# Twenty slots in place of seventeen in the shared pool, and a smaller scratch region for dynamic transfers

## The chip, the cores and the metric

The kernel runs on one core of one Trainium2 chip. The metric is the device time of one execution in microseconds (us), the median of several runs. Engines are named as the profile names them: PE (matrix products), PEld (its weight loads), DVE (vector), ACT (scalar), POOL (GpSimd) and SP (which here issues DMA transfers).

## The reference

Two layers work on 512 tokens of 1024 channels in float32. Layer 0 mixes tokens with RWKV-7, layer 1 with a spatial gating unit (SGU); a SwiGLU network (FFN, 2816 hidden channels) follows each, and every sub-layer has a norm before and after it.

```python
def step(S, inp):                                   # RWKV-7, for each of 16 heads of 64 channels
    r_t, w_t, k_t, v_t, a_t, b_t = inp
    sa = jnp.einsum('bhij,bhj->bhi', S, a_t)
    S = (S * w_t[:, :, None, :]
         + sa[..., None] * b_t[:, :, None, :]
         + v_t[..., None] * k_t[:, :, None, :])
    y = jnp.einsum('bhij,bhj->bhi', S, r_t)
    return S, y
...
for i in range(DEPTH):                              # DEPTH = 2
    h = _rmsnorm(x, norm_gains[i, 0])
    h = _rwkv7_time_mix(h, ...) if i % N_MIXERS == 0 else _sgu_mixer(h, ...)
    x = x + _rmsnorm(h, norm_gains[i, 1])
    h = _rmsnorm(x, norm_gains[i, 2])
    h = (jax.nn.silu(h @ w_gate) * (h @ w_up)) @ w_down
    x = x + _rmsnorm(h, norm_gains[i, 3])
```

## The kernel before

The four sub-layers run one after the other: RWKV from 0 to about 430 us, FFN0 to about 690, SGU to about 960, FFN1 to the end at 1313.6. Every large product is made of three matmuls (`mm3`, L206): the float32 operands are split into a high half (cast on ACT, L181, `whi`) and a low half (subtraction on DVE, L182, `wlo`).

RWKV handles the heads in four blocks of four heads (256 channels). Instead of a loop over tokens it takes chunks of 64 tokens. A string fixes in which order the steps are written down, and a scheduler of the language then sets the order on each engine from what depends on what, so that the steps overlap:

```python
PLAN = "P0 E0 P1 E1 P2 E2 P3 E3 X0 F0 B0 F1 V0 V1 V2 V3 B1 S0 F2 S1 F3 N0 B2 N1 B3 S2 N2 S3 N3".split()
```

The letters that matter here, each with the number of its block:

- X prepares the mixed input of the v-projection (`xsp`, four buffers of the shared pool), and V is that projection (`v`, PE, L206); its results go to memory (`Vd`, L868).
- F ("front") loads `MV` (L988) and `ST` (L982), multiplies them (`lm`, PE, L1004) and transposes `ST` (`bkt`, PE, L1018). ACT copies the results into `MV`, `BX` and `LA`, POOL masks them (L972).
- B ("back") inverts triangular matrices. DVE transposes `LA` to `LX` (L1035), runs 15 steps that fill `Dm` (`tm`, L1049, and `Dm`, L1051), and transposes `Dm` twice (`hn` L1054 and `Dt` L1055). Then PE and the copying engines alternate: `Qp` (PE, L1071), `Qs` (DVE, L1074), `Np` and `Tp` (PE, L1080, L1083), `Dn` (ACT, L1086), `bdT` (ACT and DVE, L1088), `Q2p` (PE, L1094), `Q` (ACT and DVE, L1097, L1098), `T2p` (PE, L1103), `bdT` (ACT and DVE, L1107). At its end PE makes `mp` (L1112) and `gh` (L1119), and DVE writes eight pairs of `MV` from them (L1121, L1122). PE also transposes `MV` in it (`mvt`, L1062).
- S scans the eight chunks: `us` and `Yp` on PE (L1148, L1161), the next state `su` on DVE and ACT (L1150, L1153), its v part loaded from `Vd` on SP (L1133).
- N finishes a block: group norm (`mu` L1177, `Y` L1179, `va` L1183, `nr` L232 to L237, `Y` L1185), the bonus (`hn`, L1195, `vt`, PE, L1198), the output gate (`g2x` L1212, `g2l` L182, `yt`, PE, L1223, `ob` on DVE, L1224 and L1228). The finished `ob` goes to memory (`od`, L1237) and comes back as `oraw` (L1281), which is split into `oT` (L181, L182) for the output projection.

Below, "block 2" means B2, the second block counted from 0 being B1; `mp(2)` is block 2's first `mp`.

Many tiles of all sub-layers share one pool of equal buffers ("slots", 4 KB in each of the 128 partitions):

```python
    def slot(self, shape, dt, name, tag="s"):
        ...
        return self.sp.tile(shape, dt, name=name, tag="s", bufs=SLOTS)
```

From this pool come four `MV` and four `BX` for each block (`BX` is free at the end of B, `MV` at the end of S), the four `xsp`, `oraw` and `oT`, the eight `hT` that each norm writes, and in an FFN its activations (`act`) and the blocks of its down projection (`ablk`, `actw`). A tile that finds no free slot is written only after the last reader of the slot's earlier tile. X0, F0 and F1 together ask for 4 + 8 + 8 = 20.

POOL issues nine transfers itself, with 512 KB each (the rows `gain` of the norms, L243, and `wsr`, L1306). For such transfers the program keeps a scratch region in every partition, 16,384 bytes by default. All other transfers are issued by SP.

Of the kernel before, what the change touches and what calls it, by code (L numbers as in the profile page):

```python
# [29 lines left out]
BANKS_F0 = dict(tr=(1, 2), gu=(3, 4, 7, 6), R=(3, 4), Q=(5, 0), Z=(7, 6), h0=(1, 2, 4, 0), h1=(3, 5, 7, 6))  # L30
BANKS_SGU = dict(tr=(1, 2), pa=(3, 5, 7, 6), h0=(1, 2, 4, 0), h1=(3, 5, 7, 6))
BANKS_F1 = dict(tr=(1, 2), gu=(4, 0, 7, 6), R=(4, 0), Q=(3, 5), Z=(7, 6), h0=(1, 2, 0, 5), h1=(4, 3, 7, 6))
SLOTS = 17
E2 = 7
PLAN = "P0 E0 P1 E1 P2 E2 P3 E3 X0 F0 B0 F1 V0 V1 V2 V3 B1 S0 F2 S1 F3 N0 B2 N1 B3 S2 N2 S3 N3".split()
XV = "xxxessss"
# [96 lines left out]
class Trunk:  # L133
# [41 lines left out]
    def slot(self, shape, dt, name, tag="s"):  # L175
        if tag == "x":
            return self.sx.tile(shape, dt, name=name, tag="x", bufs=XSLOTS)
        return self.sp.tile(shape, dt, name=name, tag="s", bufs=SLOTS)

# [1252 lines left out]
```

## Time and profile before

| what | value |
|---|---|
| median of 3 runs | 1320.23 us (1316.43 to 1321.08) |
| the profiled execution | 1315.28 us, span 1313.6 us, mean PE clock 0.984 |
| PE busy | 1257.4 us (96%) |
| DVE busy | 988.1 us (75%) |
| ACT busy | 739.4 us (56%) |
| POOL busy | 151.6 us (12%) |
| transfers issued by POOL | 1296 packets, 4.72 MB |

The times of the trace are counted from the start of the span. A row of the timeline gives start, duration, engine, line, operation, output and inputs, the number of instructions and, in brackets, how long the engine had been idle before and what ended that. A row of the windows gives for a stretch its length, the busy time of PE, PEld, DVE, ACT and POOL with the number of instructions, the clock that was granted to PE (1.00 is full), the share of the DMA engines and GB/s. In the PE rows one `lm` of the program shows as two instructions.

### The profile page before, as it was taken

To read this page: it belongs to the slowest core of one execution; us is meant where nothing else is said; L and a number is where in the kernel's file an instruction comes from. 1 tells how busy PE (TensorE), PEld (TensorE's weight loads), DVE (VectorE), ACT (ScalarE), POOL (GpSimd) and SP (SyncE) were. 2 spreads that over 40 slices of the span, in tenths; PEclk is the share of its full clock that TensorE was granted. 3 is DMA by queue.
4 is the path that set the end of the run, shared out by engine and by line. 5 is a ranking of instruction groups with operands and counts; after the bars stand their busy time and mean duration, and the time that the engine had idled before them with its cause. 6 is when DMAs were issued, how large, how long until landed. Compare 5 with 4: busy or idle time off the path is not lost.

```text
span 1313.6 us, 24404 instructions
## 1 busy us (share of the span) xinstructions
PE 1257.4 (96%) x9644; PEld 1091.1 (83%) x9644; DVE 988.1 (75%) x1613; ACT 739.4 (56%) x1303; POOL 151.6 (12%) x300
## 2 busy tenths in 40 slices
PE   5999999989899899999999999999989999999998
PEld 3667799978787698999997878878888999998876
DVE  7976766477866687868779977476679877789985
ACT  7986785686444463445546556543454454556553
POOL 0000284566000002100000000020002000000000
PEclk9999999999979999999999999999989999999999
DMA  5137594322243225244344314343430433444322
GB/s 163 34 95 175 146 224 156 88 72 65 75 127 112 75 80 160 68 126 125 92 154 136 122 49 128 94 135 94 144 97 1 129 98 105 120 125 149 113 65 81
DMA packets 219379, 144.29 MB, mean 110 GB/s; under 512 B 67920, under 2 KB 193408, under 8 KB 219264
## 3 DMA queue, kind: packets, MB, share of 16 engines
q1 hardware_dynamic: 217968, 138.01, 36.4%
q0 software_dynamic: 1296, 4.72, 1.1%
q8 instruction: 76, 1.25, 0.4%
q14 instruction: 39, 0.32, 0.1%
HBM read 128.54 MB, written 14.16 MB: 109 GB/s over the span
## 4 chain that ended last, share of the span: by engine, by line
PE 68%; DVE 7%; ACT 2%; issue 1%; DMA 1%; POOL 0%; DVEq 0%; ACTq 0%
PE acc L206 25%; PE Q L206 10%; PE gu L206 9%; PE R L206 7%; PE Z L206 7%; PE u L206 3%; DVE wlo L182 1%; PE gh L1119 1%; PE mp L1112 1%; PE Yp L1161 1%; PE lm L1004 1%; DVE wsum L405 1%; DVE x L336 1%; PE s L1366 1%; PE ptr L281 0%
## 5 line engine op out<-in xcount | busy, mean ns | idle before, releaser
L182 DVE TENSOR_TENSOR wlo<-wraw,whi 128x1024 fp32r<-128x1024 f32 x83 | 103.1, 1244 | 66.5 <-ACT whi L181 57.7
L206 PE MATMUL Q<-bc,whi 128*128 128x256 f32 x816 | 147.3, 281 | 2.2 <-ACT hn L449 2.2
L206 PE MATMUL acc<-whi,ablk 128*128 128x512 f32 x448 | 141.6, 395 | 2.7 <-DVE acc L623 2.7
L181 ACT CAST whi<-wraw 128x1024 fp32r<-128x1024 f32 x83 | 86.9, 1050 | 101.5 <-PE acc L206 29.2
L206 PEld LDWEIGHTS Q<-bc,whi 128*128 128x128 f32 x816 | 125.5, 189 | 2.8 <-ACT hn L449 2.6
L181 ACT CAST whi<-wsum 128x1024 fp32r<-128x1024 f32 x68 | 71.1, 1051 | 85.0 <-PE Q L206 24.3
L206 PE MATMUL gu<-hT,whi 128*128 128x256 f32 (+1 forms) x448 | 112.0, 342 | 3.3 <-ACT hT L62 1.7
L206 PE MATMUL Q<-bc,wlo 128*128 128x256 f32 x408 | 114.6, 281 | 0.0
L206 PEld LDWEIGHTS acc<-whi,ablk 128*128 128x128 f32 x448 | 84.2, 188 | 23.3 <-ACT hn L621 1.8
L206 PE MATMUL Z<-bc,whi 128*128 128x256 f32 x544 | 99.8, 281 | 0.0
L206 PE MATMUL R<-bc,whi 128*128 128x256 f32 x544 | 98.7, 281 | 0.0
L182 DVE TENSOR_TENSOR wlo<-wsum,whi 128x1024 fp32r<-128x1024 f32 x68 | 82.2, 1221 | 21.5 <-ACT whi L181 20.4
L181 ACT CAST whi<-wq 128x1024 fp32r<-128x1024 f32 x51 | 53.5, 1050 | 72.3 <-PE R L206 22.9
L206 PEld LDWEIGHTS gu<-hT,whi 128*128 128x128 f32 x448 | 78.8, 197 | 13.7 <-ACT hT L62 2.4
L206 PE MATMUL acc<-wlo,ablk 128*128 128x512 f32 x224 | 88.5, 395 | 1.5 <-DVE wlo L182 1.5
L182 DVE TENSOR_TENSOR wlo<-wq,whi 128x1024 fp32r<-128x1024 f32 x51 | 65.3, 1284 | 27.6 <-ACT whi L181 27.4
L206 PEld LDWEIGHTS Z<-bc,whi 128*128 128x128 f32 x544 | 84.1, 189 | 0.0
L206 PEld LDWEIGHTS R<-bc,whi 128*128 128x128 f32 x544 | 83.8, 188 | 0.2
L206 PE MATMUL proj<-xsp,whi 128*128 128x512 f32 x256 | 82.4, 401 | 1.3 <-ACT r L813 1.3
L206 PEld LDWEIGHTS Q<-bc,wlo 128*128 128x128 f32 x408 | 77.2, 189 | 0.0
L206 PE MATMUL Z<-bc,wlo 128*128 128x256 f32 x272 | 76.3, 282 | 0.9 <-DVE wlo L182 0.9
L206 PE MATMUL R<-bc,wlo 128*128 128x256 f32 x272 | 76.6, 282 | 0.0
(377 smaller groups left out, 3191.7 us busy)
## 6 DMA issues: line engine op xcount, KB each, us to landing
wc<-in_ffn_w_down_dram SPq DMA_DIRECT2D x38, 512.0 KB, 3.9
wq<-in_ffn_w_gate_dram SPq DMA_DIRECT2D x68, 256.0 KB
wq<-in_ffn_w_up_dram SPq DMA_DIRECT2D x68, 256.0 KB, 4.7
wraw<-in_rwkv_w_rkv_dram SPq DMA_DIRECT2D x24, 512.0 KB, 5.3
wraw<-in_sgu_w_in_dram SPq DMA_DIRECT2D x16, 512.0 KB, 4.3
wraw<-in_ffn_w_gate_dram SPq DMA_DIRECT2D x10, 512.0 KB
wraw<-in_ffn_w_up_dram SPq DMA_DIRECT2D x10, 512.0 KB, 3.9
x<-in_x_dram SPq DMA_DIRECT2D x8, 512.0 KB, 3.6
```

The lines of the kernel that those rows point to most:

```text
L181: self.nc.scalar.copy(hi, src)
L182: self.nc.vector.tensor_tensor(lo, src, hi.bitcast(F32), op=ALU.subtract)
L206: self.nc.tensor.matmul(out, l, r, start=start, stop=stop, skip_group_check=resumed)
L336: v.scalar_tensor_tensor(xts[tt][:, c], f, y[:, 0:1], xts[tt][:, c], op0=ALU.mult, op1=ALU.add)
L405: v.tensor_tensor(s, x, y, op=ALU.add)
L1004: mm(lm[:, cc * P:(cc + 1) * P], st[:, cc].rearrange("p n t -> p (n t)"), mv[:, cc, :, hd, :], start=True, stop=True)
L1112: mm(mp[:, cc * P:(cc + 1) * P], bdT[:, q * NC + 4 * hh + cc].rearrange("p h t -> p (h t)"), mt[:, cc, :], start=True, stop=True)
L1119: mm(gh[:, cc * P:(cc + 1) * P], mt[rows, cc, :], bx[rows, 0:2, cc, :], start=True, stop=True)
L1161: mm(yp[yr, yc], MV[hh, q][:, cc, 1, hd, :], su[:, q, hd, :], start=True, stop=True)
L1366: mm(acc[:, tt * P:(tt + 1) * P], vt[tt][:, m * P:(m + 1) * P], wsT[:, m, :], start=True, stop=True)
```

## The change

Two numbers change: the pool has 20 slots, and the scratch region has 4,096 bytes in each partition. The region gives up 12 KB of a partition, and three more slots take 12 KB.

```diff
-SLOTS = 17
+SLOTS = 20
...
-    nc = bacc.Bacc("TRN2", target_bir_lowering=False, num_devices=1)
+    nc = bacc.Bacc("TRN2", target_bir_lowering=False, num_devices=1, dynamic_dma_scratch_size=4096)
```

No operation is added or removed, but the scheduler sets another order from about 200 us on. Three places follow.

DVE behind block 0's inversion, before. `bdT<-T2p` is the end of the inversion, the `MV` pairs follow `gh`, and `LX` opens block 1.

```order
L1098 COPY Q_1947<-Q2p 32x512
L1107 COPY bdT<-T2p 32x16x32
L1121 TENSOR_TENSOR MV<-gh,BX 128x4x64
L1122 TENSOR_TENSOR MV<-gh,MV 128x4x64
L1121 TENSOR_TENSOR MV<-gh,BX 128x4x64
L1122 TENSOR_TENSOR MV<-gh,MV 128x4x64
L1121 TENSOR_TENSOR MV<-gh,BX 128x4x64
L1122 TENSOR_TENSOR MV<-gh,MV 128x4x64
L1035 STREAM_TRANSPOSE LX<-LA 128x1024
```

The same place in the changed program:

```order
L1098 COPY Q_1947<-Q2p 32x512
L1107 COPY bdT<-T2p 32x16x32
L1035 STREAM_TRANSPOSE LX<-LA 128x1024
L1049 TENSOR_TENSOR tm<-LX,Dm 128x2x15
L1051 TENSOR_TENSOR Dm<-Dm,tm 128x2x15
```

`LX` of block 1 now follows `bdT` directly, ahead of all eight `MV` pairs of block 0.

DVE at block 2, before, from the last transpose of `Dm`. The `LX` near the end is that of block 3, `ob` and `g2x` belong to N0 and N1, `su` to the scan of block 1.

```order
L1054 STREAM_TRANSPOSE hn<-Dm 128x32x32
L1055 STREAM_TRANSPOSE Dt<-Dm 128x32x32
L1228 TENSOR_TENSOR ob<-gate,ob 128x512
L1212 TENSOR_TENSOR g2x<-g2r,g2x 32x256
L1150 TENSOR_TENSOR su<-us,pc 64x2x64
L1074 TENSOR_TENSOR Qs<-Qp,id_144 128x512
L182 TENSOR_TENSOR g2l<-g_4806,g2h 128x256
L1150 TENSOR_TENSOR su<-us,pc 64x2x64 x3
L1035 STREAM_TRANSPOSE LX<-LA 128x1024
```

The same place in the changed program:

```order
L1055 STREAM_TRANSPOSE Dt<-Dm 128x32x32
L1150 TENSOR_TENSOR su<-us,pc 64x2x64
L1035 STREAM_TRANSPOSE LX<-LA 128x1024
L1228 TENSOR_TENSOR ob<-gate,ob 128x512
L1212 TENSOR_TENSOR g2x<-g2r,g2x 32x256
L1049 TENSOR_TENSOR tm<-LX,Dm 128x2x15
L1051 TENSOR_TENSOR Dm<-Dm,tm 128x2x15
L1150 TENSOR_TENSOR su<-us,pc 64x2x64
L1049 TENSOR_TENSOR tm<-LX,Dm 128x2x28
L1051 TENSOR_TENSOR Dm<-Dm,tm 128x2x14x2
L1049 TENSOR_TENSOR tm<-LX,Dm 128x2x39
L1074 TENSOR_TENSOR Qs<-Qp,id_144 128x512
```

Block 3's `LX` and its first steps now stand ahead of block 2's `Qs`.

PE at the end of block 2's inversion, before, up to its first `mp`:

```order
L1018 MATMUL bkt<-ident,ST 128x128 x4
L1094 MATMUL Q2p<-Dn_4024,LA 32x32
L1062 MATMUL mvt<-ident,MV 128x128 x4
L1094 MATMUL Q2p<-Dn_4024,LA 32x32 x18
L1062 MATMUL mvt<-ident,MV 128x128 x8
L1103 MATMUL T2p<-bdT,Q_4064 32x32 x19
L1062 MATMUL mvt<-ident,MV 128x128 x4
L1103 MATMUL T2p<-bdT,Q_4064 32x32 x13
L1198 MATMUL vt<-ident,hn 128x128 x4
L1062 MATMUL mvt<-ident,MV 128x128 x8
L1198 MATMUL vt<-ident,hn 128x128 x4
L1112 MATMUL mp<-MVt,bdT 128x128 x4
```

The same place in the changed program:

```order
L1083 MATMUL Tp<-Dt,Qs 32x32 x64
L1094 MATMUL Q2p<-Dn_4024,LA 32x32 x32
L1198 MATMUL vt<-ident,hn 128x128 x4
L1103 MATMUL T2p<-bdT,Q_4064 32x32 x32
L1198 MATMUL vt<-ident,hn 128x128 x4
L1112 MATMUL mp<-MVt,bdT 128x128 x4
```

The `mvt` and the last `bkt` have moved ahead of `Tp`; eight `vt` are what is left between its steps. From this `mp` on the rest of RWKV keeps its order on PE. In the same way the last 12 `lm` and 8 `bkt` of F1 move from behind block 0's first `mp` into the v-projection ahead of it, and on SP six loads of block 2's `MV` (L988) now stand ahead of the last two stores of `Vd`. The down projections of both FFNs keep more blocks of their input at once, and the first gate and up products of FFN1 stand in another order among the transposes (`ptr`, L281) of its norm.

## Prediction

> **What bounds the kernel now.** I read the page first, for the engine that carries the chain, then windows by stage, for the stages in which that engine is not full.
>
> ```profile
> span 1313.6 us, 24404 instructions
> PE 1257.4 (96%) x9644; PEld 1091.1 (83%) x9644; DVE 988.1 (75%) x1613; ACT 739.4 (56%) x1303; POOL 151.6 (12%) x300
> PE 68%; DVE 7%; ACT 2%; issue 1%; DMA 1%; POOL 0%; DVEq 0%; ACTq 0%
> 240.00:289.00 49.00, 44.34 (x807) 39.57 (x806) 32.12 (x73) 35.95 (x91) 31.91 (x76) 0.97 0.37 104
> 460.00:690.00 230.00, 227.51 (x1710) 217.35 (x1711) 181.03 (x238) 112.05 (x169) 15.86 (x12) 0.99 0.40 115
> 950.00:980.00 30.00, 26.39 (x170) 24.00 (x169) 25.69 (x94) 19.19 (x63) 2.36 (x4) 0.89 0.41 117
> 1190.00:1280.00 90.00, 88.68 (x400) 72.28 (x400) 85.24 (x105) 53.89 (x74) 0.00 (x0) 1.00 0.34 103
> ```
>
> PE is busy 1257.4 of 1313.6 us and no instruction is added or removed, so the change can only move the 56.2 us in which PE is idle, and the stretches in which its clock is below 1. The order changes only from about 200 us on. In the stages with a new order PE is idle 2.5 us (FFN0), 3.6 (into FFN1), 1.3 (down projection of FFN1), and 4.7 in the 49 us that hold RWKV's blocks 0 and 1. Slots are missed in one place:
>
> ```profile
> SPq L988 <- DVE MV L1121: 23.5, 5, 11.3
> ```
>
> SP's loads of `MV` wait 23.5 us, up to 11.3 at once, until DVE has written block 0's `MV` and so freed `BX`. For PE that matters where its queue runs dry or slows:
>
> ```profile
> 225.00:230.00 5.00, 3.31 (x241) 3.03 (x241) 1.37 (x2) 1.73 (x3) 0.00 (x0) 1.00 0.14 54
> 230.00:235.00 5.00, 5.00 (x56) 4.83 (x51) 0.70 (x1) 1.89 (x4) 2.00 (x5) 0.66 0.01 3
> 285.00:290.00 5.00, 4.44 (x24) 4.29 (x24) 4.55 (x9) 4.12 (x9) 3.48 (x7) 0.66 0.00 0
> ```
>
> Idle are 1.7 us at 225 to 230; the clock of 0.66 costs (1 - 0.66) x 5 = 1.7 us in each of the other two.
>
> **The scratch region: 0.** It serves only the transfers that POOL issues.
>
> ```profile
> q0 software_dynamic: 1296, 4.72, 1.1%
> L243 POOL DMA_DIRECT2D gain<-in_norm_gains_dram x4: 528/606/691, 387.5 to 1173.1; - x4
> ...
> L243 POOL DMA_DIRECT2D gain<-in_sgu_ln_b_dram x1: 528/528/528, 860.6 to 860.6; - x1
> L243 POOL DMA_DIRECT2D gain<-in_sgu_bs_dram x1: 577/577/577, 870.5 to 870.5; - x1
> ```
>
> There are nine, moving 1.1% of the engines' time, and two close ones are 870.5 - 860.6 = 9.9 us apart. If a smaller region made POOL wait before each until the last had gone, it would wait in idle time (12% busy). If it split a transfer in two, one would cost a second issue, 0.6 us, hidden there. Bounds 0 and 9 x 0.6 = 5.4 if every one were exposed; I take 0, since POOL has 88% to spare.
>
> **Blocks 0 and 1: PE gets up to 8 us ahead.** Rows of DVE and PE before:
>
> ```profile
> 236.80 0.69 DVE L1107 COPY bdT<-T2p 32x512 f32<-32x512 f32 x1 [4.99 <-ACT bdT L1107]
> 243.47 0.42 DVE L1121 TENSOR_TENSOR MV<-gh,BX 128x256 f32<-128x256 f32 x1 [5.99 <-PE gh L1119]
> 250.42 1.98 DVE L1035 STREAM_TRANSPOSE LX<-LA 128x1024 f32<-128x1024 f32 x1
> 236.07 0.66 PE L1018 MATMUL bkt<-ident,ST 128*128 128x128 f32 x4
> 281.23 2.09 PE L1004 MATMUL lm<-MV,ST 128*128 128x128 f32 x16
> 285.56 1.77 PE L1112 MATMUL mp<-MVt,bdT 128*128 128x128 f32 x8 [2.24 <-DVE bdT L1107]
> ```
>
> F1's last 12 `lm` (24 instructions at 2.09/16 = 0.13 us: 3.1) and 8 `bkt` (0.66/4 = 0.165: 1.3) move into the v-projection, 4.4 us. So block 0's `bdT` ends at 236.80 + 0.69 + 4.4 = 241.9 at the latest, and `LX` of block 1 starts right there, with `LA` already made, instead of at 250.42: 8.5 us earlier, or 10.1 if the 1.7 us gap takes part of the 4.4. `LX` leads to `mp(1)` at 285.56 in 35.1 us, and on the way PE drops 16 of F2's instructions, 2.1 us. `mp(1)` then comes at 275 to 277. PE cannot gain more than its idle 4.7 and 1.7 and the two clock losses, 2 x 1.7: 9.8. I take 8.
>
> **Block 2: most of it is given back, because DVE is full.**
>
> ```profile
> 289.00:313.10 24.10, 24.10 (x304) 20.67 (x303) 22.54 (x57) 13.94 (x36) 14.52 (x34) 0.99 0.22 54
> 288.63 1.38 DVE L1185 TENSOR_TENSOR Y<-Y,nr_y 128x1024 f32<-128x1024 f32 x1
> 290.32 1.98 DVE L1035 STREAM_TRANSPOSE LX<-LA 128x1024 f32<-128x1024 f32 x1 [0.31 <-POOL LA L972]
> 292.34 0.42 DVE L1121 TENSOR_TENSOR MV<-gh,BX 128x256 f32<-128x256 f32 x1
> 298.26 0.41 DVE L1122 TENSOR_TENSOR MV<-gh,MV 128x256 f32<-128x256 f32 x1
> 311.18 1.93 DVE L1055 STREAM_TRANSPOSE Dt<-Dm 128x1024 f32<-128x1024 f32 x1
> 312.97 0.67 DVE L1228 TENSOR_TENSOR ob<-gate,ob 128x512 f32<-128x512 f32 x1
> 313.66 0.43 DVE L1212 TENSOR_TENSOR g2x<-g2r,g2x 32x256 fp32r<-32x256 f32 x1
> 315.17 0.69 DVE L1074 TENSOR_TENSOR Qs<-Qp,id 128x512 f32<-128x512 f32 x1 [0.76 <-PE Qp L1071]
> 328.23 0.69 DVE L1088 COPY bdT<-Tp 32x512 f32<-32x512 f32 x1
> 337.38 0.69 DVE L1107 COPY bdT<-T2p 32x512 f32<-32x512 f32 x1
> 338.12 1.16 PE L1112 MATMUL mp<-MVt,bdT 128*128 128x128 f32 x8 [0.52 <-DVE bdT L1107]
> ```
>
> Four `MV` pairs of block 1 now precede `LX` of block 2 on DVE. Before, the fourth pair ended at 298.67, 13.1 us behind `mp(1)`; added to 275 to 277 that gives 288.1 to 290.1 for `LX(2)`: 1.2 us gained of 290.32 in the middle, and not 8. From `LX(2)` to the end of `Dt` took 313.11 - 290.32 = 22.8. Out go four pairs (8 x 0.37 = 3.0), in come the last steps of N0's norm (1.4 for `Y`, about 1.2 for five small ones): 22.4. `Dt` ends at 289.1 + 22.4 = 311.5, 1.6 earlier.
>
> Then `Qs` waits behind `LX` of block 3 (2.0), `ob` (0.7), `g2x` (0.4), two `su` (0.6) and five small `tm`, `Dm` (0.2, 0.2, 0.4, 0.2, 0.5): 5.2, to 316.7, where it stood at 315.17, 1.5 later. Here the price is the order itself, since `Qp` is early. From `Qs` to the second `bdT` (L1088) DVE has by the new order 24 instructions, whose durations in the trace sum to 13.4 with `Qs`, where before it took 328.92 - 315.17 = 13.75: 330.1. From there to `bdT` (L1107) stand 6.1 us, where before 338.07 - 328.92 = 9.2 went, because N1's norm now comes earlier. `bdT` ends at 336.2, 1.9 us earlier, and `mp(2)` with it. I take -2; the bounds are -8 (all that PE gained is kept) and +2 (`Qs` alone decides).
>
> **Behind `mp(2)`: 0.** The order on PE is unchanged and PE is full.
>
> ```profile
> 338.10:356.50 18.40, 17.74 (x168) 15.22 (x168) 17.70 (x45) 7.03 (x17) 0.00 (x0) 1.00 0.10 33
> 356.50:380.00 23.50, 20.16 (x541) 17.74 (x540) 9.17 (x17) 11.66 (x26) 0.41 (x2) 0.64 0.35 97
> 365.00:370.00 5.00, 4.92 (x100) 4.56 (x102) 2.44 (x5) 2.27 (x6) 0.41 (x2) 0.50 0.02 4
> ```
>
> A new hole is the price to bound: `mvt` and `bkt` no longer fill block 2's inversion, so PE stands idle there while DVE works: 24 `mvt` alone, at `bkt`'s 0.165, are 4.0 us. If the clock is 0.66 for 5 us behind it, as it was at 230, that is 1.7; if nothing, 0. The clock of these rows bears on it: 0.66 follows a short gap at 229, 0.50 stands at 365 where PE is busy 4.92 of 5.
>
> [...]
>
> **The other stages: -0.5.** In FFN0's down projection and at the start of FFN1 PE waited for what more slots might bring earlier:
>
> ```profile
> 706.65 0.50 PE L206 MATMUL acc<-wlo,ablk 128*128 128x512 f32 x1 [1.45 <-DVE wlo L182]
> 960.12 0.66 PE L281 MATMUL ptr<-ident,x 128*128 128x128 f32 x4 [2.50 <-DVE hT L64]
> ```
>
> The first waits for a weight, which no slot brings: 0, bounds -1.5 and +2 (by the 1.3 us idle in FFN1's twin, doubled for a worse order). In the second more `gu` products stand ahead of the transposes; -0.5, bounds -2.5 and +2.
>
> Sum: 0 - 2 + 0 - 0.5 = -2.5 on the profiled execution's 1315.28 us, 1312.8. The median shown is 4.95 us above that execution; on it the sum gives 1317.7, rounded 1317.5. A difference of 0.5%, 6.6 us, is about what a measurement of this kernel can tell from none.
>
> **Rivals.** (a) The lead of 8 us is kept. For it speaks that PE carries 68% of the chain and DVE waited 4.99 and 5.99 us at block 0; against it the 22.54 of 24.1 us of DVE. It needs DVE to catch up at block 2 by letting the norm's rows overlap; with the 9.8 of the bound and 0.5 it gives 1320.2 - 9 = 1311.
>
> (b) Slower: the round trip of `ob`. On ACT and DVE the two splits of block 0's `oT` now stand inside block 2's inversion, ahead of the `bdT` copy, and wait for a transfer there and back.
>
> ```profile
> 353.66 0.68 DVE L1228 TENSOR_TENSOR ob<-gate,ob 128x512 f32<-128x512 f32 x1
> 361.79 1.14 ACT L181 CAST oT<-oraw 128x512 fp32r<-128x512 f32 x2 [2.80 <-DMA oraw<-od]
> ```
>
> In block 1's trip 361.79 - 354.34 = 7.5 us passed. Block 0's second `ob` ends at about 314.6 by the steps above, so `oraw` is there at 322.1; DVE reaches `oT` 7 us behind `Qs`, at 323.7. With 1.6 us to spare it costs nothing; each us more is a us on `mp(2)`. If the load queues behind SP's loads of `su` as long as the longest wait above, 11.3, mp(2) is 9.7 later: 1320.2 - 2.5 + 9.7 = 1327.
>
> (c) Nothing comes of the slots: DVE's order costs at `Qs` what was gained, and the hole's clock takes the rest: -2 + 1.7, 1320.
>
> **Chances.** Forecast 0.42, (c) 0.20, (a) 0.25, (b) 0.13. Faster by over 0.5%: (a), and a little of the forecast's own spread, 0.28; slower: (b), 0.13; within: 0.59. The range takes in (a) with the full 9.8 and some of (b): 1308 to 1325. The likeliest case alone spans 1314 to 1321.
>
> **What would show it.** Right: `LX` of block 1 at 240 to 242, no wait of L988 for `MV`, `mp(1)` at 275 to 277, `Qs(2)` at 316 to 318, `mp(2)` at 335 to 337, PE idle ahead of it for 4 us or more. Wrong: `mp(2)` before 332 (a), ACT waiting for `oraw` before it (b), or a wait of POOL ahead of L243, for the scratch.

## The result: 0.8% slower

| | before | after |
|---|---|---|
| median | 1317.94 us (5 runs, 1314.71 to 1321.08) | 1328.10 us (5 runs, 1326.07 to 1330.81) |
| profiled execution: span, mean PE clock | 1313.6 us, 0.984 | 1324.3 us, 0.979 |
| PE idle in the span (1 minus busy) | 56.2 us | 62.9 us |

The ratio is 1.0082 with a 95% interval of 1.0064 to 1.0100: the changed kernel lies 10 us behind, outside the range of 1308 to 1325, and on the other side of the old time from the 1317.5 forecast.

The page of the changed kernel gives busy times that are almost those of before. Nothing was added; the time went into idling and into a slower clock.

```profile
span 1324.3 us, 24399 instructions
PE 1261.4 (95%) x9644; PEld 1095.7 (83%) x9644; DVE 987.7 (75%) x1613; ACT 737.9 (56%) x1303; POOL 151.7 (11%) x300
PE 76%; DVE 12%; ACT 5%; issue 3%; DMA 2%; SPq 1%; POOL 0%; DVEq 0%; ACTq 0%
```

In the chain that ended last, DVE has risen from 7% to 12%, ACT from 2% to 5% and issue from 1% to 3%. That rise is no sign of the loss: the shares before add up to 79% only, because that chain could be followed back no further than to 270 us, and the one after reaches the start. Where the time went is read from the same marks in both traces. The last mark is the start of the last product of RWKV's output projection.

| us from the start of the span | before | after | later by |
|---|---|---|---|
| `LX` of block 1 (DVE) | 250.4 | 243.4 | -7.0 |
| last `su` of block 0's scan (DVE) | 271.6 | 287.1 | 15.5 |
| first `mp` of block 1 (PE) | 285.6 | 287.1 | 1.5 |
| `LX` of block 2 (DVE) | 290.3 | 300.8 | 10.5 |
| `Qp` of block 2 (PE), first to last | 311.4 to 315.1 | 321.8 to 327.8 | 10.4 to 12.7 |
| `Qs` of block 2 (DVE) | 315.2 | 328.7 | 13.5 |
| first `mp` of block 2 (PE) | 338.1 | 346.0 | 7.9 |
| last product of RWKV's output projection | 453.9 | 463.7 | 9.8 |
| end of the span | 1313.6 | 1324.3 | 10.7 |

The lead of 7 us that the prediction expected at block 1's `LX` is there. It is gone at block 1's `mp`, has become a loss of 10 at block 2's `LX`, and all but 0.9 of the loss has arisen by the end of RWKV. How far such marks scatter is seen in the traces of the first two experiments below, in which RWKV has the order of before: `LX` of block 2 at 292.6 and 290.5, `mp` of block 2 at 341.1 and 338.5, the last product at 456.3 and 465.0. So less than 3 us at a mark of block 1 or 2 tells nothing, and at the last product one trace can be 11 us late without a new order. That the loss itself is there rests on the medians of the runs. Two places explain the rows up to block 2's `mp`.

**First place: the scan of block 0 and block 1's inversion in one queue.** `Qp` of block 1 needs `hn`. From `LX` to the end of `hn` DVE takes 18.1 us before and 18.3 after, but before, `Qp` begins 0.2 us behind that end,

```profile
266.42 2.12 DVE L1054 STREAM_TRANSPOSE hn<-Dm 128x1024 f32<-128x1024 f32 x1
268.69 1.28 PE L1071 MATMUL Qp<-hn,LA 32*32 32x32 f32 x128 [0.47 <-DVE hn L1054]
271.61 0.28 DVE L1150 TENSOR_TENSOR su<-us,pc 64x128 f32<-64x128 f32 x1 [0.56 <-ACT su L1153]
```

and after, at 266.65, 5.0 us behind it: on PE a `Yp` of block 0's scan stands ahead of `Qp` and waits for `su`, which stands on DVE behind `hn` and `Dt`, and 16 `lm` follow.

```profile
259.65 2.03 DVE L1054 STREAM_TRANSPOSE hn<-Dm 128x1024 f32<-128x1024 f32 x1
263.31 0.25 DVE L1150 TENSOR_TENSOR su<-us,pc 64x128 f32<-64x128 f32 x1
263.61 0.33 PE L1161 MATMUL Yp<-su,MV 128*64 128x64 f32 x2 [2.00 <-DVE su L1150]
263.87 2.85 PE L1004 MATMUL lm<-MV,ST 128*128 128x128 f32 x16
```

The timeline of DVE after, from block 1's `LX` on: the scan's last states and what ended DVE's wait for them, then block 1's `MV` pairs and block 2's `LX`.

```profile
243.38 2.04 DVE L1035 STREAM_TRANSPOSE LX<-LA 128x1024 f32<-128x1024 f32 x1 [1.72 <-POOL LA L972]
278.42 0.28 DVE L1150 TENSOR_TENSOR su<-us,pc 64x128 f32<-64x128 f32 x1 [2.07 <-PE us L1148]
284.23 0.28 DVE L1150 TENSOR_TENSOR su<-us,pc 64x128 f32<-64x128 f32 x1 [4.80 <-PE us L1148]
287.06 0.28 DVE L1150 TENSOR_TENSOR su<-us,pc 64x128 f32<-64x128 f32 x1 [1.84 <-PE us L1148]
291.61 0.42 DVE L1121 TENSOR_TENSOR MV<-gh,BX 128x256 f32<-128x256 f32 x1 [4.27 <-PE gh L1119]
297.77 0.42 DVE L1121 TENSOR_TENSOR MV<-gh,BX 128x256 f32<-128x256 f32 x1 [0.97 <-PE gh L1119]
298.11 0.41 DVE L1122 TENSOR_TENSOR MV<-gh,MV 128x256 f32<-128x256 f32 x1
299.57 1.28 DVE L1195 TENSOR_TENSOR hn<-hn,bn 128x512 f32<-128x512 f32 x2
300.77 1.98 DVE L1035 STREAM_TRANSPOSE LX<-LA 128x1024 f32<-128x1024 f32 x1
```

PE in the same stretch:

```profile
266.65 1.82 PE L1071 MATMUL Qp<-hn,LA 32*32 32x32 f32 x120
277.20 0.76 PE L1094 MATMUL Q2p<-Dn,LA 32*32 32x32 f32 x36 [1.91 <-issue]
277.89 0.45 PE L1148 MATMUL us<-su,MV 128*64 128x64 f32 x8
282.62 1.19 PE L1103 MATMUL T2p<-bdT,Q 32*32 32x32 f32 x62
```

DVE waits for `us`, and `us` stands on PE behind `Q2p` and `T2p` of block 1. Before, six of the scan's seven steps ran ahead of block 1's `Qp` on PE and the seventh ahead of `Np`; after, three run ahead of it and four between the steps of the inversion, which begins 7 us earlier. Each chain needs the answer of another engine after every step, and in one queue it also waits for the other's answers and for the `lm` between them. `LX` to `mp` of block 1 takes 43.7 us in place of 35.1, and the scan ends 15.5 us later.

`LX` of block 2 then begins 13.7 us behind block 1's `mp`, where it began 4.8 us behind it. Three things come ahead of it: four `MV` pairs of block 1 that now stand ahead of it on DVE, the last of them released by `gh` at 297.77; two instructions of block 0's norm (`va`, `hn`), which starts only behind its scan; and block 2's `LA`, whose last mask ended at 297.2 and not at 290.3, since F2's `lm` stand in the same queue of PE. This trace doesn't tell which of the three would do alone.

**Second place: block 2's filling work ahead of its inversion.** In the changed kernel `mvt` and the last `lm` and `bkt` stand before or between the pieces of `Qp`, which takes 6.0 us and not 3.7. Its first and last pieces before,

```profile
311.38 0.89 PE L1071 MATMUL Qp<-hn,LA 32*32 32x32 f32 x80
...
314.74 0.38 PE L1071 MATMUL Qp<-hn,LA 32*32 32x32 f32 x20
```

and after, with some of the `mvt`:

```profile
321.20 0.60 PE L1062 MATMUL mvt<-ident,MV 128*128 128x128 f32 x4
321.81 0.73 PE L1071 MATMUL Qp<-hn,LA 32*32 32x32 f32 x62
...
323.86 0.66 PE L1062 MATMUL mvt<-ident,MV 128*128 128x128 f32 x4
...
327.42 0.38 PE L1071 MATMUL Qp<-hn,LA 32*32 32x32 f32 x20
```

Behind `Qp` PE runs dry:

```profile
335.66 0.25 PE L1083 MATMUL Tp<-Dt,Qs 32*32 32x32 f32 x3 [1.96 <-issue]
340.43 1.12 PE L1198 MATMUL vt<-ident,hn 128*128 128x128 f32 x4 [3.26 <-DVE hn L1195]
345.99 2.07 PE L1112 MATMUL mp<-MVt,bdT 128*128 128x128 f32 x8 [1.28 <-DVE bdT L1107]
```

For the gap of 1.96 us the trace shows nothing that PE waited for ("issue"). Such gaps stand in runs of 32x32 products of the kernel before, too (1.53 us at 229.46, 1.47 at 364.48), so its reason stays open; at the other two PE waits for DVE.

The windows of 5 us from 335, first before, then after:

```profile
335.00:340.00 5.00, 4.20 (x26) 3.72 (x24) 4.77 (x16) 1.96 (x3) 0.00 (x0) 0.79 0.02 3
340.00:345.00 5.00, 4.64 (x39) 3.94 (x40) 4.80 (x17) 1.10 (x2) 0.00 (x0) 1.00 0.00 0
345.00:350.00 5.00, 5.00 (x47) 4.24 (x46) 4.96 (x10) 2.08 (x4) 0.00 (x0) 1.00 0.13 52
```

```profile
335.00:340.00 5.00, 1.51 (x67) 1.37 (x66) 4.94 (x10) 2.11 (x3) 0.00 (x0) 0.66 0.41 122
340.00:345.00 5.00, 4.08 (x72) 3.21 (x72) 4.87 (x17) 2.19 (x5) 0.00 (x0) 0.50 0.02 3
345.00:350.00 5.00, 4.01 (x18) 3.68 (x19) 4.77 (x10) 1.03 (x2) 0.00 (x0) 0.50 0.00 0
```

PE idles 3.5 us of the first stretch while DVE is full (4.94 of 5), and for the 10 us behind it the granted clock is half. The eight instructions of `mp` take 2.07 us, where they took 1.16 before. Idle time, and busy time multiplied by what the clock lacks to 1, come to 10.0 us between 335 and 350 (5.4 and 4.6), and in the kernel before to 2.0. That is an estimate from the mean clocks of these windows, but it is most of the 10 us. From `Qs` to `mp` the changed kernel is the faster one, 17.3 us against 23.0, since the filling work is done by then.

### The profile page after: what moved, and what is told of

The parts are those of the page before. It is cut to its first block, busy times and chain, and to the rows that moved or that the text cites. A ratio compares the mean times of both kernels' runs of the same rounds, so it can differ in the third digit from the quotient of the medians.

```text
span 1324.3 us, 24399 instructions
## 1 busy us (share of the span) xinstructions
PE 1261.4 (95%) x9644; PEld 1095.7 (83%) x9644; DVE 987.7 (75%) x1613; ACT 737.9 (56%) x1303; POOL 151.7 (11%) x300
## 4 chain that ended last, share of the span: by engine, by line
PE 76%; DVE 12%; ACT 5%; issue 3%; DMA 2%; SPq 1%; POOL 0%; DVEq 0%; ACTq 0%
PE acc L206 22%; PE Q L206 9%; PE gu L206 9%; PE R L206 7%; PE Z L206 6%; PE proj L206 5%; PE u L206 3%; PE v L206 2%; PE lm L1004 2%; DVE wlo L182 2%; PE gh L1119 2%; PE mp L1112 1%; PE Yp L1161 1%; ACT whi L181 1%; ACT xs L765 1%
## 5 line engine op out<-in xcount | busy, mean ns | idle before, releaser
L206 PEld LDWEIGHTS gu<-hT,whi 128*128 128x128 f32 x448 | 78.8, 197 | 13.5 <-DVE hT L64 2.6
```

Of the source, the lines that this page charges most:

```text
L206: self.nc.tensor.matmul(out, l, r, start=start, stop=stop, skip_group_check=resumed)
```

## The experiments

The kernels of one group ran on one chip, with runs of the kernel before among them; ratios are to those. In the diffs `issue_after(x)` places what it wraps behind `x` in the queue of `x`'s engine, without a wait for its result, and the scheduler orders the rest anew. `hold()` takes three slots of the pool for idle tiles, and `release()` gives them back.

**The two parts of the change.** One kernel has only the small scratch region:

```diff
-SLOTS = 20
+SLOTS = 17
```

> The small scratch region alone, with 17 slots; the order of every instruction on every engine is that of before. If the region costs nothing (first theory, and what the prediction said): ratio to before 1.000, within 0.002. If the smaller region makes POOL's nine transfers wait (rival): up to the whole 1.008, with a wait ahead of the loads of L243 on POOL that the trace of before does not have.

Measured: 1.0003 (0.9983 to 1.0023). The region costs nothing that can be measured.

The other keeps 20 slots but takes three away until the end of RWKV:

```diff
+            hold()
             g_hidden()
...
+            release()
             oT = {}
```

> Twenty slots, of which three are held by idle tiles until the end of RWKV, so that RWKV has the order of before and FFN0, SGU and FFN1 have that of the changed kernel. First theory (the loss arises in RWKV, between 200 and 350 us): ratio 1.000, at most 0.002 off; the traces put the changed kernel's RWKV 7.9 us behind at block 2's mp and the rest of it at 10. Rival (the down projections and FFN1's start are worse in the new order): 1.003 or more.

Measured: 1.0001 (0.9983 to 1.0018). The whole loss belongs to RWKV. (Its profiled execution, 1326.6 us, is not a typical one: the median of its 12 runs is 1317.25. The last section comes back to it.)

**Attempts to take one cause away.** My first theory was the second place alone. Two kernels were to tell it from the effects of F1.

```diff
+                if n == 'F2':
+                    hold()
...
+            release()
             oT = {}
```

> Twenty slots up to F1, and from F2 to the end of RWKV three of them held by idle tiles. On PE everything up to block 1's last mp keeps the order of the changed kernel, but 4 bkt and 24 mvt stay behind block 2's Qp, between its steps. First theory (the filling work of block 2, drawn ahead of Qp, delays Qp and leaves a hole behind it, in which PE idles and its clock falls): of the 10 us about 5 to 7 come back, ratio 1.002 to 1.004, clock 1.0 behind block 2's mp. Rival (what F1 changes at blocks 0 and 1 is the whole loss): 1.008 stays.

Measured: 1.0090 (1.0070 to 1.0109). The rival's number. Block 2's `LX` comes at 304.0, later still than in the changed kernel, and its `Qp` takes 3.6 us, as before: what F1's slots alone set off at blocks 0 and 1 is enough for the whole loss.

```diff
-                MVt = {}
-                for hh in range(2):
...
+                if b == 2:
+                    with self.tc.issue_after(last.ins):   # Tp's last
+                        turn()                            # the mvt and their copies
```

> Twenty slots, and only block 2's 24 mvt are held behind its Tp on PE; on PE the order up to block 2's Qp is that of the changed kernel, and DVE still has block 3's LX ahead of block 2's Qs. First theory (the hole): 24 mvt at 0.165 us fill 4 us of the hole, Qp ends up to 4 us sooner, and the clock does not fall: 4 to 7 us come back, ratio 1.003 to 1.005. Rival (the order on DVE, with block 3's LX, ob and small steps, 5.2 us, ahead of Qs, sets block 2's mp): at most 1 us comes back, ratio 1.007 to 1.008.

Measured: 1.0194 (1.0168 to 1.0221), against both. The filling work was put back, but into the wrong spots, as PE's rows of this kernel show:

```profile
341.42 1.11 PE L1064 MATMUL mvt<-ident,MV 128*128 128x128 f32 x4 [2.69 <-ACT MVt L1067]
353.05 1.22 PE L206 MATMUL gate<-sg,g2h 128*128 128x512 f32 x2 [3.13 <-DVE ob L1232]
```

An `mvt` that waits 2.69 us for ACT's copy of an earlier one stands in the middle of `Q2p`, and a `gate` that waits for `ob` stands ahead of `mp`, which begins at 354.9. In these spots the filling work itself had to wait. So this run says nothing on the size of the hole.

**The second theory: the scan.** Four kernels.

```diff
+                with ExitStack() as order:
+                    if b == 1:
+                        order.enter_context(self.tc.issue_after(ops[0]["paired"].ins))   # block 0's last MV
                     v.transpose(full(LX), ...)
```

> Twenty slots, and only block 1's LX is held behind block 0's last MV pair on DVE, as it stood before. On PE block 0 keeps the order of the changed kernel (F1 early), the scan of block 0 is through its steps ahead of block 1's Qp again, and block 2's mvt still stand ahead of its Np. Theory now (block 1's inversion, started 7 us sooner, gets in front of the last four steps of block 0's scan on PE and DVE; the norm of block 0 and block 2's LX come 10 us late by it): block 2's LX at 288 to 294 and not 301, ratio 0.999 to 1.003. First theory (the hole in block 2 by the early mvt): that is left as it is, 1.006 to 1.009. Rival (F1's products ahead of block 0's Qp, which comes 3.7 us late): 1.003 to 1.005.

```diff
-... V3 B1 S0 F2 ...
+... V3 S0 B1 F2 ...
...
+                    if b == 1:
+                        order.enter_context(self.tc.issue_after(ops[0]["us"].ins))
                     (Qp's loop)
```

> Twenty slots, the scan of block 0 written ahead of block 1's inversion, and block 1's Qp held behind the scan's last us on PE; LX of block 1 stays early on DVE. Theory now (scan behind inversion): as in the run with the late LX, or better by what the early LX brings: 0.996 to 1.003. Rival (only the time at which LX of block 1 runs matters, since DVE is the bound): as the changed kernel, 1.006 to 1.009. First theory (hole in block 2): 1.006 to 1.009.

```diff
-SLOTS = 20
+SLOTS = 18
```

> Eighteen slots, small scratch region. F1's last products stay behind block 0's first mp as before, four of the scan's seven steps stand ahead of block 1's Qp (before seven, in the changed kernel three), and block 2's mvt stand ahead of its Np as in the changed kernel. First theory (hole in block 2): 1.005 to 1.008. Theory now (scan behind inversion): between, 1.003 to 1.007, with block 2's LX at 293 to 299. Rival (F1's early products): 1.000 to 1.002.

```diff
+                    if b == 3:
+                        order.enter_context(self.tc.issue_after(ops[2]["qs"].ins))
                     v.transpose(full(LX), ...)
```

> Twenty slots, and only block 3's LX is held behind block 2's Qs on DVE; blocks 0 and 1 and PE up to block 2's Tp are those of the changed kernel. If the 5 us ahead of Qs on DVE count (what the prediction priced at 1.5 us late): 2 to 5 us come back, ratio 1.004 to 1.007. Theory now (the loss arises ahead of block 2's LX, and Qp of block 2 is late anyway): at most 2 us, 1.007 to 1.009.

Measured, with the marks of each trace:

| kernel | ratio | `LX` block 2 | `Qp` block 2 | `mp` block 2 |
|---|---|---|---|---|
| late `LX` of block 1 | 1.0160 (1.0134 to 1.0186) | 296.2 | 325.1 to 333.8 | 351.4 |
| `Qp` of block 1 behind the scan | 1.0166 (1.0138 to 1.0194) | 293.7 | 326.2 to 334.2 | 351.7 |
| 18 slots | 1.0130 (1.0092 to 1.0169) | 299.5 | 320.7 to 330.6 | 348.1 |
| late `LX` of block 3 | 1.0127 (1.0100 to 1.0155) | 302.6 | 323.7 to 329.7 | 347.9 |

Every expectation on the time failed: all four ratios are above the changed kernel's 1.0082, those of the last two not clear of it. The first two did not restore the order that they were meant to restore. In the kernel before only three of block 0's eight `MV` pairs stand ahead of block 1's `LX`; the edit put it behind all eight, at 262.7 in place of 250.4. The second put `Qp` of block 1 behind the scan's last step, at 277.5 in place of 268.7. So both brought a delay of their own: block 1's `mp` begins at 301.5 and 299.1, where it began at 287.1 in the changed kernel and at 285.6 before.

With the scan ahead of the inversion again, `LX` of block 2 gains 4.6 to 7.1 us on the changed kernel's 300.8 (in the first of the two not quite into the range I gave). But `Qp` of block 2 then begins 3 to 4 us later than in the changed kernel and takes 8 to 9 us, with other work between its pieces. I took this for a second cause that had been hidden behind the first; the new delay at block 1 is a rival that these two runs don't exclude. The late `LX` of block 3 gained nothing, though `Qs` of block 2 then followed the end of `Qp` at once and not 0.9 us behind it. So DVE's order ahead of `Qs`, which the prediction priced at 1.5 us, is not what matters.

**Each cause alone, and both away.** If two causes stand in a row, each must cost something when it alone is put into the order of before. For the filling work first by force, in the kernel before:

```diff
+                    if b == 2:
+                        order.enter_context(self.tc.issue_after(o["mvt"].ins))
                     (Qp's loop)
```

> The kernel before (17 slots, default scratch) with one change: block 2's Qp is held on PE behind its mvt, so that the last lm and bkt of F2 and F3 and 16 of 24 mvt stand ahead of Qp, the other eight between Qp and Np, and only eight vt between the later steps of the inversion. Blocks 0 and 1 keep the order of before. Theory of the filling work in block 2 (drawn ahead of Qp it delays Qp and leaves a hole behind it): Qp 6 to 10 us later, ratio 1.003 to 1.008, though LX of block 2 is at 290 as before. Theory of the scan behind block 1's inversion alone: 1.000 to 1.001.

Measured: 1.0101 (1.0084 to 1.0118), just above the range I gave. `Qp` begins at 330.8, 19.4 us late and more than expected, because it also waits for the `mvt` themselves.

Then, from the other side, kernels with 20 slots in which the causes are taken away:

```diff
     (late LX of block 1 as above)
+                if n == 'F2':
+                    hold()
```

> Twenty slots up to F1; block 1's LX is held behind block 0's last MV pair on DVE, and from F2 on three slots are held by idle tiles, so that in block 2 the lm, bkt and mvt stand between the steps of the inversion as before. F1's products stay ahead of block 0's Qp and mp. If the loss has two causes in a row (the scan behind block 1's inversion, and the filling work ahead of block 2's Qp), each of which alone costs about as much as both: 0.999 to 1.004, where the late LX alone gave 1.016 and the held slots alone 1.009. If F1's early products are a third cause: 1.003 to 1.006. If neither order matters: 1.009 to 1.016.

```diff
+                for n, (hh, q) in enumerate(units):
+                    with ExitStack() as order:
+                        if b == 1 and n > 1:
+                            order.enter_context(self.tc.issue_after(ops[0]["mp"][3].ins))
+                        unit(hh, q)                       # lm, bkt and their copies
...
+                if n == 'F2':
+                    hold()
```

> As the run before, but block 1's LX is left free and instead 16 of F1's lm and 8 bkt are held behind block 0's first mp on PE, where about that many stood before. Scan and block 1 come in the order of before by that, and block 2 nearly. Two causes in a row: 0.999 to 1.003, close to the kernel before. Otherwise 1.009 or more.

```diff
     (F1's last units as above, nothing held)
```

> Twenty slots throughout, and only the 16 lm and 8 bkt of F1 are held behind block 0's first mp. Blocks 0 and 1 and the scan keep nearly the order of before, in block 2 the mvt stand ahead of Np as in the changed kernel. Two causes in a row: LX of block 2 at 290 to 294, then Qp late by the filling work: 1.004 to 1.010. Only the scan: 0.999 to 1.002.

| kernel | ratio | `LX` block 2 | `Qp` block 2 | `mp` block 2 |
|---|---|---|---|---|
| late `LX` of block 1, slots held | 1.0205 (1.0186 to 1.0225) | 295.2 | 322.8 to 332.2 | 354.8 |
| F1 late, slots held | 1.0059 (1.0042 to 1.0076) | 292.6 | 316.6 to 323.8 | 345.9 |
| F1 late | 1.0106 (1.0088 to 1.0124) | 295.2 | 319.0 to 331.3 | 347.2 |

The first is the worst of all and missed every expectation: it has the same new delay as the late `LX` alone (block 1's `mp` at 302.5), `Qp` still takes 9.4 us there, and block 3's `LX` falls to 347.6. The second wins back part of the loss, less than I had expected; its `Qp` still takes 7.2 us. The third, with the scan in nearly its old place, lands just above the range that the filling work alone should give. The whole order of before with 20 slots gave 1.0001; of the half-way orders tried none came nearer than 1.0059.

The last two kernels each put one cause by itself into the order of before. F1 and F2 with 17 slots, F3 with 20:

```diff
+            hold()
             g_hidden()
...
+                if n == 'F3':
+                    release()
```

> Twenty slots, of which three are held by idle tiles until F3: F1 and F2 have seventeen, so that blocks 0 and 1 and the scan of block 0 keep the order of before, and F3's lm and bkt and block 2's mvt come ahead of block 2's Np. Filling work as a cause of its own: LX of block 2 at 290 to 294, Qs of block 2 at 323 to 332 in place of 315, ratio 1.004 to 1.010. If the scan behind block 1's inversion is the only cause: 1.000 to 1.002.

Measured: 1.0102 (1.0075 to 1.0130). The timeline of PE shows the pieces of `Qp` and what stands between them:

```profile
314.51 0.43 PE L1071 MATMUL Qp<-hn,LA 32*32 32x32 f32 x26
315.34 1.16 PE L1004 MATMUL lm<-MV,ST 128*128 128x128 f32 x8
...
321.09 0.73 PE L206 MATMUL gate<-sg,g2h 128*128 128x512 f32 x2
322.12 0.60 PE L1062 MATMUL mvt<-ident,MV 128*128 128x128 f32 x4
...
325.70 0.26 PE L1071 MATMUL Qp<-hn,LA 32*32 32x32 f32 x8
...
337.22 1.92 PE L1103 MATMUL T2p<-bdT,Q 32*32 32x32 f32 x64 [2.36 <-ACT bdT L1088]
```

and the windows what follows:

```profile
335.00:340.00 5.00, 2.78 (x68) 2.50 (x68) 4.87 (x11) 2.40 (x5) 0.00 (x0) 0.51 0.14 49
340.00:345.00 5.00, 3.85 (x17) 3.34 (x17) 4.73 (x18) 2.36 (x4) 0.00 (x0) 0.50 0.00 0
345.00:350.00 5.00, 3.76 (x32) 3.14 (x31) 4.97 (x7) 0.58 (x1) 0.00 (x0) 0.97 0.00 0
```

`LX` of block 2 comes at 293.0 and `Dt` is ready at 312.8, as before (313.1); then `Qp` is spread over 11.5 us and `Qs` comes at 326.1 in place of 315.2. The scan has no part in that. But the late `Qs` is not handed on: `mp` of block 2 begins at 341.3, level with the 341.1 of the scratch kernel, which loses nothing. Of the 12.5 us by which this trace's last product is late against the kernel before (466.4), 9.3 arise behind that `mp`. Nor does the run part the filling work from the other moves from F3 on: `LX` of block 3 stands ahead of `Qs` here too, at 321.0.

And the kernel before, where the edit moves nothing but the scan's last four steps:

```diff
+                        with ExitStack() as order:
+                            if b == 0 and c > 2:
+                                order.enter_context(self.tc.issue_after(
+                                    ops[1][{3: "qp", 4: "q2p"}.get(c, "t2p")].ins))
                             (us of the scan's step c)
```

> The kernel before (17 slots, default scratch) with the last four steps of block 0's scan held on PE behind block 1's Qp, Q2p and T2p, where they stand in the changed kernel; F1 keeps its place. If the scan behind block 1's inversion is a cause of its own: LX of block 2 at 296 to 302 in place of 290, and ratio 1.004 to 1.012. If LX of block 2 comes late only by F1's early products: LX at 290 to 293, ratio 1.000 to 1.003.

Measured: 1.0093 (1.0068 to 1.0118). `LX` of block 2 is at 294.9, short of the 296 to 302 expected; the last `su` of the scan at 282.7 (271.6), `Dt` ready at 322.4, `Qs` at 325.0 and `mp` at 347.4, 9 us late. Block 1's inversion loses nothing by it (`mp` at 282.7, 2.9 us sooner). `LX` of block 2 had its `LA` at 288.4 and stood behind the four `MV` pairs of block 1, which the new order puts ahead of it on DVE, as in the changed kernel. The hole is there too, in PE's timeline:

```profile
347.39 2.08 PE L1112 MATMUL mp<-MVt,bdT 128*128 128x128 f32 x8 [3.85 <-DVE bdT L1107]
```

and in its windows:

```profile
335.00:340.00 5.00, 2.35 (x54) 1.96 (x49) 4.77 (x11) 2.23 (x4) 0.00 (x0) 1.00 0.01 3
340.00:345.00 5.00, 2.76 (x70) 2.08 (x66) 4.62 (x13) 1.35 (x3) 0.00 (x0) 0.66 0.01 3
345.00:350.00 5.00, 2.61 (x10) 2.52 (x11) 3.05 (x3) 0.45 (x1) 0.00 (x0) 0.50 0.00 0
```

So each of the two alone costs 0.9 to 1.0%, as much as both together in the changed kernel (0.8%). What they have in common is the hole with the low clock. Worked out as above, idling and clock between 335 and 350 come to 8.0 us and 9.5 us here, to 10.0 in the changed kernel and to 2.0 before. That this hole is the common cause fits these sums, but it is not shown: no run takes the hole away by itself, and the kernel with F1 late and slots held has 8.2 us there at a ratio of 1.0059.

Not clean is that the scheduler of the last kernel also moved block 2's `mvt` about; what of its 0.9% is the scan's lateness and what the new order behind it is not told apart. Nor is it shown which of the two a partial repair of the changed kernel would have to remove first. No kernel tried beats the one before.

## Why the prediction was wrong

- **The scratch region, 0: right.** 1.0003.
- **Blocks 0 and 1, `LX` of block 1 at 241.9 or sooner: nearly right,** 243.4; it waited 1.72 us for the mask of its `LA`. **"`LX` leads to `mp(1)` in 35.1 us": this step failed.** It took 287.1 - 243.4 = 43.7. I moved the inversion forward as a block and subtracted F2's work from its path, but did not list what else lay in PE's queue there: the scan's steps, which the earlier inversion now overtook, and `lm` between them. Of the 8.6 us, 5.0 lie between the end of `hn` and `Qp` and 3.5 between `Qp` and `mp(1)`. The forecast of 275 to 277 was missed by 10 to 12 us.
- **Block 2, `LX(2)` at 288 to 290: failed by consequence,** 300.8. The step itself held: 13.1 us behind `mp(1)` by the prediction, 13.7 measured. That DVE is full, and that block 2 gives the lead back, was right in direction and far too small.
- **The steps within block 2 were sized well,** if counted from the late start: from `LX` to the end of `Dt` 23.4 us (22.4 forecast), from there to `Qs` 4.5 (5.2), and from `Qs` to the last `bdT` 17.3 (19.5). The second was in part luck: it rests on an early `Qp`, and `Qp` ended only 0.9 us ahead of `Qs`. They are no help when the start is 11 us off.
- **Behind `mp(2)`, 0: wrong by 1.9** in this pair of traces (9.8 against 7.9 at the end of the output projection). The hole was named and priced at 0 to 1.7 us; by the windows, the clock in it and behind it cost 1.51 x 0.34 + 8.09 x 0.50 = 4.6 us of PE's time between 335 and 350, where the kernel before lost 4.20 x 0.21 = 0.9. In windows of half a us the clock is 1.00 up to 336.5, 0.61 up to 337.0 and 0.50 from there to 350.0. So it fell about 1 us behind the end of the gap of 1.96 us, and ahead of the gap of 3.26 us. The 1.7 us took one row of before, 5 us at 0.66, for the hole; measured were 13 us at 0.50.
- **The other stages, -0.5: right within what can be measured** (1.0001 with RWKV in the old order; 0.9 us in the one pair of traces).
- **Rivals.** The 1327 of rival (b) is nearly the measured time, but not by its mechanism: ACT's row for the two splits has no wait for `oraw`. (The sum of rival (a) is off by itself: 9.8 and 0.5 are 10.3, which gives 1309.9 and not 1311.)

```profile
333.73 1.14 ACT L181 CAST oT<-oraw 128x512 fp32r<-128x512 f32 x2
```

The right rival would have been "the earlier chain overtakes another chain in the same queue"; the order of the changed program showed it, on PE, before any run.

## What to carry to other kernels

More buffers do not only let work start earlier, they let a scheduler put it somewhere else: before trusting the gain, list for each engine's queue what now stands between the steps of every chain that waits for other engines. A chain that shares a queue with another can wait for the other's answers (here `Qp` of block 1 began 5.0 us behind `hn`, and not 0.2), and filling work that is drawn ahead of a chain is missing where the chain waits (here PE idled 3.5 of the 5 us from 335, and before 0.8). A pool's size is then a setting of the order like any other, to be tried (17, 18 and 20 gave 1.000, 1.013 and 1.008 here) and not reasoned upward.

## What was unexpected of the hardware

The granted clock goes with much of the spread and a good part of the loss. Over 81 executions of kernels with RWKV's old order the span falls by 0.79 us for each 0.001 of mean clock (a fitted line, which takes up 60% of the variance). The changed kernel's five runs have a mean clock of 0.9766 against 0.9829 there, which by that line stands for 5.0 of the 10 us. That is an estimate from a line, and it can't be parted from the idling, since in the two traces in which the fall to 0.50 was followed it stands behind gaps of PE: 1.96 us in the changed kernel, 0.84 and 0.77 us in the trace below.

A half clock also came with RWKV in its old order, and stayed while PE was full. The profiled execution of that kernel shows it: 1.6 us of idling between 380 and 385, in two gaps of 0.84 and 0.77 us, then 20 us at 0.50 with PE busy 5.00 of every 5, where the kernel before has 1.00.

```profile
380.00:385.00 5.00, 3.39 (x20) 2.55 (x18) 2.45 (x6) 1.53 (x2) 0.00 (x0) 0.96 0.12 34
385.00:390.00 5.00, 5.00 (x28) 4.09 (x27) 2.89 (x5) 1.99 (x2) 0.00 (x0) 0.50 0.63 210
...
400.00:405.00 5.00, 5.00 (x15) 3.93 (x15) 3.37 (x9) 1.62 (x2) 0.00 (x0) 0.50 0.06 13
```

That execution was 9.4 us above its kernel's median (1326.6 against 1317.25), as much as the whole effect studied here; two traces alone could not have shown it.
